# Order of half-height matmuls in the GLA and RWKV mixers, and a full-height last product in FFN down

## The chip, the cores and the metric

The kernel runs on one NeuronCore of a Trainium2 chip. A core has five engines with a queue each: TensorE (PE, matmuls; its weight loads are shown apart as PEld), VectorE (DVE), ScalarE (ACT), GpSimd (POOL) and SyncE (SP, which here only issues DMAs). Matmuls write to PSUM, 8 banks of 128 x 512 float32; DVE and ACT read from there. The metric is the device time of one execution in microseconds. Lower is better.

## The reference

A trunk of two layers over 512 tokens with 1024 features, in float32. Layer 0 mixes with GLA (gated linear attention, chunks of 64) and RWKV-7 (chunks of 16), layer 1 with RG-LRU and mLSTM. Each layer then has a cross attention to 256 memory tokens and a gated FFN of width 2752 with a causal convolution. What the change touches, cut down:

```python
def gla_chunked(q, k, v, log_alpha):              # 4 heads, dk 64, dv 128, L = 64
    q_dec = q * exp(g); k_inv = k * exp(-g); k_end = k * exp(g_last - g)
    scores = where(causal, einsum('bhnlk,bhnsk->bhnls', q_dec, k_inv), 0.0)
    o_local = einsum('bhnls,bhnsv->bhnlv', scores, v)
    # over the chunks:  o_state = q_c @ S;  S = S * decay + k_end_c^T @ v_c
    return o_local + o_state

def rwkv7_group(...):                             # 8 heads, N = 64, L = 16
    log_w = -DECAY * sigmoid(w0 + tanh(w_lr) @ w2)
    a = sigmoid(a0 + a_lr @ a2)
    # per chunk: masked products of (a_dec, r_dec) with (b_inv, k_inv), a triangular solve, a scan

def conv_glu_ffn(xn, w_up, conv_w, conv_b, w_down):   # D_FF = 2752 = 21 * 128 + 64
    u, gt = split(xn @ w_up)
    return (silu(causal_dwconv(u)) * gt) @ w_down
```

## The kernel before, in words

Activations lie with features on partitions and the 512 tokens along the free dimension, in blocks of 128 features. A dense product takes a weight block through `wload` (L240 on): one DMA on SP's queue into a ring of three `raw` tiles, then ACT makes a high part `wh` and DVE a low part `wl`, in rings of two. `dense` multiplies both with the high and low parts of the operands (`xs`), three float32r products of 128 x 128 by 128 x 512 for each k block. These go to the PSUM pool `mm` (three banks). All other products are plain float32 and go to the pool `ax` (five banks); each float32 product is two records in the trace. Every product but the transposes is issued on line 209, so the tile names tell them apart.

The program is written as one stream of operations. A scheduler puts them on the engines' queues by data, free buffers and its own estimate of time, the written order being the priority. So dense products of a later step can stand between the products of an earlier one.

- **FFN down** (`down`, L371 on). The 22 blocks of the hidden layer are multiplied in three parts of 8, 8 and 6. The last block has only 64 real rows; its operand holds the high part on rows 0 to 63 and the low part on rows 64 to 127, and the weights' rows are there twice. So one product with `wh` makes hi\*hi and hi\*lo, and one with 64 rows of `wl` makes lo\*hi. In each layer that happens once for each of 8 output blocks; the last one of layer 1 is done in two halves of 256 tokens.
- **GLA** (`gla`). Two heads share a tile of 128 partitions (`qd`, `ki`): head `e` of pair `p` lies on rows 64e to 64e + 63. Scores (L690 on): for each head four products over 64 rows, 128 x 128, into one `ax` bank, then a masked copy on DVE into `SC`. State (L698 on): products of 64 x 64 x 128 into `us`, and a recurrence on DVE into `S`. Outputs (L714 on): for each of 4 heads one bank `o`; for each of four blocks of 128 tokens a full-height product of `v` with `SC`, then up to two half-height ones of `S` with `qd`, 64 tokens each. Then the head's norm: a square on ACT, a product with `ones_h`, Ln and Exp on ACT, a multiply on DVE.
- **RWKV** (`rwkv`, loop over `p` from L790). For each pair of heads: three blocks of the projection, the two low-rank products with `w2a2` (rows 0 to 63 for the decay, rows 64 to 127 for `a`), a chain on ACT and DVE, and the pair products (L838 on): for two groups of four chunks and each half `e`, four products over 64 rows into one bank, two masked multiplies on DVE from it, then four transposes. `during(p)` puts GLA's gate blocks and the memory's norm behind each turn. After the loop DVE solves the triangular systems.

The buffers of GLA are given back when its last head is done. The buffer of `w2a2` comes after that, and its load stands on SP's queue ahead of the later weights.

Of the kernel before, what the change touches and what calls it, by code (L numbers as in the profile page):

```python
# [17 lines left out]
P = 128  # L18
T = 512
# [123 lines left out]
class Trunk:  # L143
    def __init__(self, ctx, tc, I):
# [19 lines left out]
        for n, v in (("d", 1.0 / D), ("h", 1.0 / P)):  # L164
            t = con.tile([P, P], F32, name="ones_" + n)
            nc.gpsimd.memset(t, v)
            self.ones[n] = t
        # keeps the tensor engine at its full clock while the first loads are on their way
        warm = self.mm.tile([P, T], F32, name="mm")
# [21 lines left out]

# [1 line left out]
    def tt(self, out, a, b, op, eng=None):  # L193
# [17 lines left out]
    def conv(self, out, u, w):  # L211
        """Causal convolution of a padded tile (data from column 4); w: the taps, then the bias."""
        n = len(w) - 1
        self.act(out, u[:, 4:], AF.Identity, scale=w[n - 1], bias=w[n])
        for i in range(n - 2, -1, -1):
            d = n - 1 - i
            self.stt(out, u[:, 4 - d:T + 4 - d], w[i], out, ALU.mult, ALU.add)
# [4 lines left out]
    def split(self, pool, a):  # L222
        """hi and lo parts of a: their sum is a, and both are exact in float32r."""
        hi, lo = self.pair(pool)
        n = a.shape[0]
        self.act(hi[:n], a, AF.Copy)
        self.tt(lo[:n], a, hi[:n].bitcast(F32), ALU.subtract)
        return hi, lo

    def exp_ln(self, after=None):  # L230
        """Have the table set with both exp and ln loaded (after an instruction of ScalarE)."""
        name = "natural_log_exp_and_others"
        if after is None:
            self.nc.scalar.preload_act_table_set(name)
        else:
            with self.tc.issue_after(after.ins):
                self.nc.scalar.preload_act_table_set(name)

# [1 line left out]
    def wload(self, src, kb, m):  # L240
# [11 lines left out]
    def dense(self, ps, W, X, first=True, last=True):  # L252
        """ps += W^T X over the k blocks of W and X, each in hi and lo parts."""
        wh, wl = W
        n = len(X)
        for k, (xh, xl) in enumerate(X):
            self.mmul(ps, wh[:, k], xh, first and k == 0, False)
            self.mmul(ps, wh[:, k], xl, False, False)
            self.mmul(ps, wl[:, k], xh, False, last and k == n - 1)
# [8 lines left out]
    def half(self, name, j, k0, X, h):  # L268
        """h += the products over k blocks k0 to k0 + 3."""
        W = self.wload(self.I[name][:, j, k0:k0 + 4], 4, P)  # L270
        ps = self.mm.tile([P, T], F32, name="mm")
        self.dense(ps, W, X)
        self.add(h, h, ps)

    # ---- RMS norm: gains into the operands, 1/rms left to the consumer --
    def rstd_of(self, pool, acc, n, name, ring):
# [19 lines left out]
class Norm:  # L296
# [28 lines left out]
    def bc(self):  # L325
        """1/rms along the tokens, on all partitions."""
        if self.b is None:
            self.b = self.K.rstd_of(self.small, self.acc, self.n, "rstd", self.ps)
        return self.b

    def tok(self):
        """1/rms with the tokens on partitions."""
        if self.t is None:
# [4 lines left out]
def ffn(K, l, nm, h, feed, out=None):  # L338
    nc, X = K.nc, nm.X
    cv = lambda t, j: K.v(f"ffn_conv{l}", t * NFF + j)  # L340
    with ExitStack() as es:
# [29 lines left out]
        def down(ps, W, c, s=slice(0, T)):  # L371
# [3 lines left out]
            else:  # L375
                K.dense(ps, W, g[:-1], False, False)
                K.mmul(ps, W[0][:, 5], g[-1][0], False, False)
                K.mmul(ps, W[1][:64, 5], g[-1][0][:64], False, True)

# [104 lines left out]
def memory_norm(K, sm):  # L484
    """The normalised memory, [feature, m], two blocks of features to a tile."""
    nc = K.nc
# [32 lines left out]
def memory_k(K, l, X, stage):  # L519
    """k^T [feature, m] of layer l into DRAM; X in two parts, or whole."""  # L520
    nc = K.nc
# [17 lines left out]
def memory_v(K, l, X, stage):  # L539
    """v [m, feature] of layer l into DRAM."""  # L540
    nc = K.nc
# [23 lines left out]
def reset_mask(K, pool, n):  # L565
    """Ones, with a zero where each chunk starts."""
    t = pool.tile([P, 8, n], F32, name=f"reset{n}")
# [5 lines left out]
def stacked_weights(K, src, n, m, w, queue):  # L573
    """n columns (with zeros up to m) in hi parts, and in lo parts from column m on."""
    raw = K.wr.tile([P, 1024], F32, name="raw")[:, :KD * m]
# [8 lines left out]
def stacked_step(K, ps, w, n, k, x):  # L584
    """The products of block k: hi and lo parts of the columns land on rows from 0 and from m."""
    xh, xl = x
# [6 lines left out]
def gla(K, nm, wga, wk, squares, after, Y):  # L593
    nc, X = K.nc, nm.X
    with ExitStack() as es:
# [79 lines left out]
        for half in range(2):  # L675
# [12 lines left out]
            for t in range(4):  # L688
                K.act(v[:, t, half * 256:(half + 1) * 256], ps[t // 2][:, t % 2], AF.Copy, scale=rt[:, t:t + 1])
        for p in range(2):  # L690
            for e in range(2):
                r = slice(64 * e, 64 * e + 64)
                ps = K.ax.tile([P, 4, P], F32, name="ax")
                for t in range(4):
                    ts = slice(t * P, (t + 1) * P)
                    K.mmul(ps[:, t], ki[p][r, ts], qd[p][r, ts])
                nc.vector.copy_predicated(out=SC[2 * p + e], mask=gm.to_broadcast([P, 4, P]), data=ps)
        S = gp.tile([P, 2, 7, P], F32, name="S")  # L698
        for p in range(2):
            us = {}  # L700
            for c in range(7):
# [10 lines left out]
                else:  # L712
                    K.stt(S[:, p, c], S[:, p, c - 1], sd[p][:, c, 63:64], u, ALU.mult, ALU.add)
        for h in range(4):  # L714
            p, r = h // 2, slice(64 * (h % 2), 64 * (h % 2) + 64)
            o = K.ax.tile([P, T], F32, name="ax")
            for t in range(4):
                ts = slice(t * P, (t + 1) * P)
                K.mmul(o[:, ts], v[:, t, h * P:(h + 1) * P], SC[h][:, t], t == 0, False)
                for c in (2 * t, 2 * t + 1):  # L720
                    if c:
                        cs = slice(c * 64, c * 64 + 64)
                        K.mmul(o[:, cs], S[r, p, c - 1], qd[p][r, cs], False, c == 7)
            sq = gt.tile([P, T], F32, name="sq")
# [19 lines left out]
def shifted(K, pool, name, ps, rstd, i, out=None):  # L744
    """Token shift of a projected block: p + (prev - p) * mu."""
    u = K.u[i % 2]
# [8 lines left out]
def sigmoid(K, out, a, **kw):  # L755
    """1 / (1 + exp(-a)); scale and bias as they go into exp."""
    K.act(out, a, AF.Exp, **kw)
# [4 lines left out]
def rwkv(K, X, rstd, Y, during, after):  # L762
# [3 lines left out]
    with ExitStack() as core:  # L766
# [11 lines left out]
        with ExitStack() as es:  # L778
# [11 lines left out]
            for p in range(4):  # L790
                r = shifted(K, K.qr, "xs", K.block("w_rw", p, X), rstd, p)
                k = shifted(K, K.qr, "xs", K.block("w_rw", 4 + p, X), rstd, 4 + p)
                v = shifted(K, K.qr, "xs", K.block("w_rw", 8 + p, X), rstd, 8 + p, vp[:, 64:576])
                ps = K.ax.tile([P, T], F32, name="ax")
                K.mmul(ps, w2a2[0:64, p * P:(p + 1) * P], wa[0:64])
                e1 = tp.tile([P, 8, 65], F32, name="e1")
                nc.gpsimd.memset(e1[:, :, 0:1], 0.0)
# [9 lines left out]
                K.act(sdt[:, :, p:p + 1], e1[:, :, 64:65], AF.Copy)  # L807
                ps = K.ax.tile([P, T], F32, name="ax")
                K.mmul(ps, w2a2[64:128, p * P:(p + 1) * P], wa[64:128])
                a = tp.tile([P, T], F32, name="a")  # L810
                sigmoid(K, a, ps, scale=-1.0, bias=neg[:, 4 + p:5 + p])
                kn = tp.tile([P, T], F32, name="kn")
# [25 lines left out]
                for c0 in (0, 4):  # L838
                    cs = slice(c0, c0 + 4)
                    rm = K.rmask.rearrange("p (o m) -> p o m", o=1).to_broadcast([P, 4, P])  # L840
                    for e in range(2):
                        ps = K.ax.tile([P, 4, P], F32, name="ax")
                        for c in range(4):
                            K.mmul(ps[:, c], bk[R[e], c0 + c].rearrange("p a l -> p (a l)"),
                                   stk[e][R[e], p, c0 + c])
                        K.mul(BB[R[e], p, cs], ps[R[e]], rm[R[e]])
                        K.mul(stk[e][R[1 - e], p, cs], ps[R[1 - e]], rm[R[1 - e]])
                    ps = K.ax.tile([P, 4, P], F32, name="ax")
# [114 lines left out]
def lru(K, X, rstd, Y, after, gate):  # L963
    nc = K.nc
    with ExitStack() as es:
# [3 lines left out]
        nc.sync.dma_start(out=wg, in_=K.I["w_lg"])  # L969
        # softplus(-lam) = max(-lam, 0) + log1p(e), e = exp(-|lam|); log1p(e) = 2 atanh(e / (2 + e))  # L970
        o0 = VEC["lru_lambda"][0]
# [66 lines left out]
def mlstm(K, nm, hp):  # L1038
    nc, X = K.nc, nm.X
    with ExitStack() as es:  # L1040
# [18 lines left out]
        ch = [slice(P * c, P * c + P) for c in range(4)]  # L1059
        # gate rows: heads on partitions 0-3 (input) and 32-35 (forget)  # L1060
        wif = stacked_weights(K, K.I["w_if"][:, 0], 36, 64, K.wh.tile([P, 1024], F32R, name="wh"), nc.sync)
# [150 lines left out]
def trunk(tc, I, out):  # L1212
    nc = tc.nc
    with ExitStack() as ctx:
# [63 lines left out]
        for l in range(2):  # L1278
# [23 lines left out]
            else:  # L1302
# [3 lines left out]
                def finish(s, ps):  # L1306
                    """The last block of the residual for some tokens, their norm, and their output."""
                    r = nt.tile([P, T], F32, name="nsq")[:, 0:256]
# [29 lines left out]
```

## Time and profile before

| | us |
|---|---|
| median of 3 runs | 1587.1 |
| lowest and highest run | 1581.17, 1588.97 |
| profiled execution: span from its first to its last instruction | 1579.1 |
| PE busy in it | 1550.2 |
| DVE busy | 937.3 |
| ACT busy | 667.6 |

The page gives the profiled execution by its span alone. The runs shown are 2.1 to 9.9 us longer than that span; what lies around the span, ahead of the first and behind the last instruction, is within this difference. The mean granted clock of TensorE over the span is 0.992 of full speed. A share of busy time is a mean over stages; PE's records overlap, so the length of a stretch of PE is read from the starts of its records.

### The profile page before, as it was taken

To read this page: it belongs to the slowest core of one execution; us is meant where nothing else is said; L and a number is where in the kernel's file an instruction comes from. 1 tells how busy PE (TensorE), PEld (TensorE's weight loads), DVE (VectorE), ACT (ScalarE), POOL (GpSimd) and SP (SyncE) were. 2 spreads that over 40 slices of the span, in tenths; PEclk is the share of its full clock that TensorE was granted. 3 is DMA by queue.
4 is the path that set the end of the run, shared out by engine and by line. 5 is a ranking of instruction groups with operands and counts; after the bars stand their busy time and mean duration, and the time that the engine had idled before them with its cause. 6 is when DMAs were issued, how large, how long until landed. Compare 5 with 4: busy or idle time off the path is not lost. (4 is left out here: it accounts for less than half of the span.)

```text
span 1579.1 us, 19936 instructions
## 1 busy us (share of the span) xinstructions
PE 1550.2 (98%) x7953; PEld 1249.7 (79%) x7953; DVE 937.3 (59%) x1382; ACT 667.6 (42%) x1058; POOL 23.3 (1%) x62
## 2 busy tenths in 40 slices
PE   8999998999999999999999999999999999999997
PEld 6877777786888888888877767788888888888776
DVE  6447989646555756655633375777567655565233
ACT  5345542436444543333322257565445333333221
POOL 2000000011000000000000000000000000000000
PEclk9999999899999999999999999999999999999999
DMA  5212225335341333333333330325214333333332
GB/s 175 68 47 94 67 72 150 120 90 195 117 131 36 100 107 93 94 96 104 91 97 90 91 109 28 91 63 153 74 47 120 95 99 100 94 93 97 94 93 77
DMA packets 50173, 152.17 MB, mean 96 GB/s; under 512 B 5504, under 2 KB 8864, under 8 KB 50080
## 3 DMA queue, kind: packets, MB, share of 16 engines
q1 hardware_dynamic: 45664, 142.87, 30.0%
q10 hardware_dynamic: 3536, 5.38, 0.9%
q0 software_dynamic: 880, 2.66, 0.5%
q8 instruction: 62, 1.02, 0.3%
q14 instruction: 31, 0.25, 0.0%
HBM read 144.59 MB, written 6.29 MB: 96 GB/s over the span
## 5 line engine op out<-in xcount | busy, mean ns | idle before, releaser
L209 PE MATMUL mm<-xs,wh 128*128 128x512 f32 (+1 forms) x3627 | 1114.8, 388 | 3.2 <-DVE upad L194 1.4
L209 PEld LDWEIGHTS mm<-xs,wh 128*128 128x128 f32 x3627 | 670.6, 188 | 150.6 <-issue 10.4
L209 PE MATMUL mm<-xs,wl 128*128 128x512 f32 (+2 forms) x1814 | 702.6, 387 | 0.3 <-DVE wl L194 0.3
L206 ACT ACTIVATE wh<-raw 128x1024 fp32r<-128x1024 f32 (+2 forms) x273 | 264.9, 970 | 537.6 <-PE mm L209 438.7
L194 DVE TENSOR_TENSOR wl<-raw,wh 128x1024 fp32r<-128x1024 f32 (+2 forms) x272 | 302.5, 1112 | 192.7 <-ACT wh L206 191.8
L209 PEld LDWEIGHTS mm<-xs,wl 128*128 128x128 f32 (+1 forms) x1814 | 341.0, 188 | 77.7 <-issue 7.6
L194 DVE TENSOR_TENSOR upad<-mm,rstd 128x512 f32<-128x512 f32 x66 | 45.5, 690 | 111.2 <-PE mm L209 108.0
L194 DVE TENSOR_TENSOR h<-h,mm 128x512 f32<-128x512 f32 (+1 forms) x73 | 49.4, 677 | 72.5 <-PE mm L209 72.4
L194 DVE TENSOR_TENSOR g<-mm,rstd 128x512 f32<-128x512 f32 (+1 forms) x44 | 30.4, 692 | 76.0 <-PE mm L209 75.9
L209 PE MATMUL mm<-wh,xs 128*128 128x256 f32 (+1 forms) x256 | 67.3, 350 | 0.7 <-ACT wh L206 0.7
L203 DVE SCALAR_TENSOR_TENSOR c<-upad,vec,c 128x512 f32<-128x512 f32 (+1 forms) x88 | 65.9, 749 | 3.3 <-ACT c L206 1.8
L206 ACT ACTIVATE c<-c 128x512 f32<-128x512 f32 (+1 forms) x44 | 27.8, 632 | 87.1 <-DVE c L203 87.1
L209 PEld LDWEIGHTS mm<-wh,xs 128*128 128x128 f32 x256 | 44.5, 192 | 8.0 <-ACT wh L206 2.3
L209 PE MATMUL mm<-wl,xs 128*128 128x256 f32 (+1 forms) x128 | 44.6, 348 | 4.5 <-DVE wl L194 4.5
L206 ACT ACTIVATE xs<-g 128x512 fp32r<-128x512 f32 (+1 forms) x44 | 27.8, 633 | 27.2 <-DVE g L194 27.2
L206 ACT ACTIVATE c<-upad,vec 128x512 f32<-128x512 f32 (+1 forms) x44 | 35.3, 802 | 1.5 <-DVE upad L194 1.5
L206 ACT ACTIVATE e<-ax,mx,scl 128x256 f32<-128x256 f32 x32 | 17.8, 560 | 39.8 <-DVE mx L194 39.8
L194 DVE TENSOR_TENSOR g<-c,g 128x512 f32<-128x512 f32 (+1 forms) x44 | 30.4, 692 | 6.1 <-ACT c L206 1.4
L194 DVE TENSOR_TENSOR nacc<-nacc,nsq 128x512 f32<-128x512 f32 x45 | 32.9, 730 | 0.3
L194 DVE TENSOR_TENSOR xs<-ax,xs 128x512 fp32r<-128x512 f32 x32 | 21.3, 687 | 18.0 <-ACT xs L206 18.0
L203 DVE SCALAR_TENSOR_TENSOR xs<-h,vec,xs 128x512 fp32r<-128x512 f32 x40 | 29.9, 749 | 3.5 <-ACT xs L206 3.4
L206 ACT ACTIVATE xs<-h,vec 128x512 fp32r<-128x512 f32 x40 | 28.9, 722 | 7.3 <-DVE h L194 6.6
(349 smaller groups left out, 1248.2 us busy)
## 6 DMA issues: line engine op xcount, KB each, us to landing
raw<-in_w_up SPq DMA_DIRECT2D x86, 512.0 KB, 3.5
raw<-in_w_dn SPq DMA_DIRECT2D x32, 512.0 KB, 3.6
raw<-in_w_kk SPq DMA_DIRECT2D x16, 512.0 KB, 4.1
raw<-in_w_kv SPq DMA_DIRECT2D x16, 512.0 KB, 4.5
raw<-in_w_q SPq DMA_DIRECT2D x16, 512.0 KB, 3.8
raw<-in_w_o SPq DMA_DIRECT2D x32, 256.0 KB, 2.7
raw<-in_w_cd SPq DMA_DIRECT2D x16, 512.0 KB, 3.6
raw<-in_w_rw SPq DMA_DIRECT2D x14, 512.0 KB, 3.8
```

Source lines behind the costliest of these rows:

```text
L194: (eng or self.nc.vector).tensor_tensor(out=out, in0=a, in1=b, op=op)
L203: return self.nc.vector.scalar_tensor_tensor(out=out, in0=a, scalar=s, in1=b, op0=op0, op1=op1)
L206: return self.nc.scalar.activation(out=out, in_=a, func=f, **kw)
L209: self.last_mm = self.nc.tensor.matmul(out, lhsT=l, rhs=r, start=start, stop=stop)
```

## The change

1. FFN down: the product of `wl` with the last block uses all 128 rows of both operands.
2. GLA scores: both heads of a pair get a bank, their products alternate, and the two masked copies follow.
3. GLA outputs: a function `outputs(p)` does two heads at a time: first all full-height products of both heads, then the half-height ones, alternating between the heads.
4. RWKV: the `a` product of `w2a2` is written right behind the decay product, into a bank of its own.
5. RWKV pair products: both halves get a bank, and their products alternate.

Comments and docstrings are dropped as well. The diff, cut to what computes:

```diff
@@ ffn
-                K.mmul(ps, W[1][:64, 5], g[-1][0][:64], False, True)
+                K.mmul(ps, W[1][:, 5], g[-1][0], False, True)
@@ gla
         for p in range(2):
+            ps = [K.ax.tile([P, 4, P], F32, name="ax") for _ in range(2)]
+            for t in range(4):
+                ts = slice(t * P, (t + 1) * P)
+                for e in range(2):
+                    r = slice(64 * e, 64 * e + 64)
+                    K.mmul(ps[e][:, t], ki[p][r, ts], qd[p][r, ts])
             for e in range(2):
-                r = slice(64 * e, 64 * e + 64)
-                ps = K.ax.tile([P, 4, P], F32, name="ax")
-                for t in range(4):
-                    ts = slice(t * P, (t + 1) * P)
-                    K.mmul(ps[:, t], ki[p][r, ts], qd[p][r, ts])
-                nc.vector.copy_predicated(out=SC[2 * p + e], mask=gm.to_broadcast([P, 4, P]), data=ps)
+                nc.vector.copy_predicated(out=SC[2 * p + e], mask=gm.to_broadcast([P, 4, P]), data=ps[e])
...
+        def outputs(p):
+            os = [K.ax.tile([P, T], F32, name="ax") for _ in range(2)]
+            for e in range(2):
+                h = 2 * p + e
+                for t in range(4):
+                    ts = slice(t * P, (t + 1) * P)
+                    K.mmul(os[e][:, ts], v[:, t, h * P:(h + 1) * P], SC[h][:, t], t == 0, False)
+            for c in range(1, 8):
+                for e in range(2):
+                    r = slice(64 * e, 64 * e + 64)
+                    cs = slice(c * 64, c * 64 + 64)
+                    K.mmul(os[e][:, cs], S[r, p, c - 1], qd[p][r, cs], False, c == 7)
+            return os
+
         for h in range(4):
-            p, r = h // 2, slice(64 * (h % 2), 64 * (h % 2) + 64)
-            o = K.ax.tile([P, T], F32, name="ax")
-            for t in range(4):
-                ts = slice(t * P, (t + 1) * P)
-                K.mmul(o[:, ts], v[:, t, h * P:(h + 1) * P], SC[h][:, t], t == 0, False)
-                for c in (2 * t, 2 * t + 1):
-                    if c:
-                        cs = slice(c * 64, c * 64 + 64)
-                        K.mmul(o[:, cs], S[r, p, c - 1], qd[p][r, cs], False, c == 7)
+            if h % 2 == 0:
+                os = outputs(h // 2)
+            o = os[h % 2]
@@ rwkv
                 ps = K.ax.tile([P, T], F32, name="ax")
+                psa = K.ax.tile([P, T], F32, name="ax")
                 K.mmul(ps, w2a2[0:64, p * P:(p + 1) * P], wa[0:64])
+                K.mmul(psa, w2a2[64:128, p * P:(p + 1) * P], wa[64:128])
...
-                ps = K.ax.tile([P, T], F32, name="ax")
-                K.mmul(ps, w2a2[64:128, p * P:(p + 1) * P], wa[64:128])
                 a = tp.tile([P, T], F32, name="a")
-                sigmoid(K, a, ps, scale=-1.0, bias=neg[:, 4 + p:5 + p])
+                sigmoid(K, a, psa, scale=-1.0, bias=neg[:, 4 + p:5 + p])
...
+                    ps = [K.ax.tile([P, 4, P], F32, name="ax") for _ in range(2)]
+                    for c in range(4):
+                        for e in range(2):
+                            K.mmul(ps[e][:, c], bk[R[e], c0 + c].rearrange("p a l -> p (a l)"),
+                                   stk[e][R[e], p, c0 + c])
                     for e in range(2):
-                        ps = K.ax.tile([P, 4, P], F32, name="ax")
-                        for c in range(4):
-                            K.mmul(ps[:, c], bk[R[e], c0 + c].rearrange("p a l -> p (a l)"),
-                                   stk[e][R[e], p, c0 + c])
-                        K.mul(BB[R[e], p, cs], ps[R[e]], rm[R[e]])
-                        K.mul(stk[e][R[1 - e], p, cs], ps[R[1 - e]], rm[R[1 - e]])
+                        K.mul(BB[R[e], p, cs], ps[e][R[e]], rm[R[e]])
+                        K.mul(stk[e][R[1 - e], p, cs], ps[e][R[1 - e]], rm[R[1 - e]])
```

## Rows read from the trace of the kernel before

**Rows 1.** The page's first part: busy us, share of the span, records.

```profile
PE 1550.2 (98%) x7953; PEld 1249.7 (79%) x7953; DVE 937.3 (59%) x1382; ACT 667.6 (42%) x1058; POOL 23.3 (1%) x62
```

**Rows 2.** Waits of PE: line, released by; us in total, times, longest.

```profile
PE ax L209 <- DVE sc L697: 0.6, 1, 0.6
```

**Rows 3.** Chain that ended last, in order of time: start, us, what.

```profile
1216.36 347.35 PE mm L209 x1552
```

**Rows 4.** Groups with shapes apart, PE: rows x columns, operand, count | busy us, mean ns | idle.

```profile
L209 PE MATMUL mm<-xs,wl 64*128 64x512 f32 x15 | 7.4, 492 | 0.0
...
L209 PE MATMUL mm<-xs,wl 64*128 64x256 f32 x2 | 0.8, 384 | 0.0
```

**Rows 5.** Timeline of PE, end of a block of FFN down: start us, us, record.

```profile
817.43 0.39 PE L209 MATMUL mm<-xs,wl 128*128 128x512 f32 x1
817.67 0.40 PE L209 MATMUL mm<-xs,wh 128*128 128x512 f32 x1
818.00 0.49 PE L209 MATMUL mm<-xs,wl 64*128 64x512 f32 x1
818.42 0.73 PE L209 MATMUL mm<-xs,wh 128*128 128x512 f32 x2
```

**Rows 6.** Timeline of PE, outputs of GLA's second head.

```profile
80.77 0.39 PE L209 MATMUL ax<-sc,v 128*128 128x128 f32 x2
81.08 0.43 PE L209 MATMUL ax<-qd,S 64*128 64x64 f32 x2
81.44 0.49 PE L209 MATMUL ax<-sc,v 128*128 128x128 f32 x2
81.86 0.66 PE L209 MATMUL ax<-qd,S 64*128 64x64 f32 x4
...
84.45 0.50 PE L209 MATMUL mm<-xs,wh 128*128 128x512 f32 x1
```

**Rows 7.** Timeline of PE, transposes of full height in RWKV.

```profile
123.89 1.20 PE L825 MATMUL ax<-cmat,vp 128*128 128x128 f32 x9 [0.27 <-DVE vp L203]
```

**Rows 8.** Timeline of PE, the low-rank products of the first p.

```profile
120.51 1.13 PE L209 MATMUL ax<-wa,w2a 64*128 64x512 f32 x4
121.57 1.12 PE L209 MATMUL ax<-kn,cmat 128*128 128x512 f32 x2
```

**Rows 9.** Timeline of PE, GLA scores.

```profile
65.09 2.82 PE L209 MATMUL ax<-qd,ki 64*128 64x128 f32 x32
```

**Rows 10.** Timeline of DVE, masked copies of the scores.

```profile
68.04 1.93 DVE L697 COPY_PREDICATED sc<-gmask,ax 128x512 f32<-128x512 uint8 x3
```

**Rows 11.** Timeline of PE, pair products of the third p, both groups.

```profile
196.91 1.94 PE L209 MATMUL ax<-stk,bk 64*128 64x128 f32 x16 [0.26 <-DVE bk L194]
...
199.37 1.71 PE L209 MATMUL ax<-stk,bk 64*128 64x128 f32 x16
```

**Rows 12.** Busy in the first p's pair products: PE, PEld, DVE, ACT, POOL, clock.

```profile
134.00:142.00 8.00, 7.44 (x52) 5.96 (x52) 7.88 (x13) 1.87 (x3) 0.00 (x0) 1.00 0.01 2
```

**Rows 13.** Timeline of PE, a wait in the second p.

```profile
155.05 0.47 PE L209 MATMUL mm<-xs,wh 128*128 128x512 f32 x1 [1.36 <-DVE upad L194]
```

**Rows 14.** Busy behind the first head's outputs, columns as in rows 12.

```profile
76.90:80.40 3.50, 3.50 (x10) 2.48 (x10) 0.00 (x0) 0.60 (x1) 0.00 (x0) 0.51 0.02 5
```

**Rows 15.** Timeline of SP, the load of w2a2.

```profile
100.21 0.33 SPq L782 DMA_DIRECT2D w2a<-in_w_w2a  x1
```

**Rows 16.** Timeline of PE, a dense product among GLA's state products.

```profile
69.78 0.51 PE L209 MATMUL mm<-xs,wh 128*128 128x512 f32 x1
70.22 0.43 PE L209 MATMUL ax<-v,kt 64*64 64x128 f32 x5
```

**Rows 17.** Timeline of PE, from one block of the projection to the next.

```profile
98.43 0.39 PE L209 MATMUL mm<-xs,wl 128*128 128x512 f32 x1
98.66 0.62 PE L209 MATMUL mm<-xs,wh 128*128 128x512 f32 x2
```

## The prediction

> **What bounds the kernel now.** I read the page first, then the waits of PE, then the chain that ended last, and only then single stretches. PE is busy for 1550.2 of 1579.1 us, so only 28.9 us of the span are free of matmul work [rows 1]. The waits say the same of the place that the change touches first: only one wait of PE, 0.6 us, is for the masked scores of GLA [rows 2]. The chain runs for its last piece, 347.35 us long, through nothing but dense products of the second FFN [rows 3]. So PE's stream sets the time nearly everywhere, and an edit that shortens the stream is worth its full length, unless the next product then waits for DVE, ACT or a load. The start times of the matmuls tell how long the stream is; busy time does not, since matmuls overlap.
>
> **FFN down.** The edit removes no instruction: 17 products that use 64 rows [rows 4] now use 128. Around one of them the starts are 817.43, 817.67, 818.00 and 818.42, and the two after it last 0.73 together, so the second of these starts at about 818.42 + 0.73 - 0.40 = 818.75 [rows 5]. The steps are 0.24 (full to full), then 0.33, 0.42, 0.33. Three steps of full height are 3 x 0.235 = 0.70, and these take 1.08: a half-height product between full ones costs 0.38 us. Fifteen of width 512 give 15 x 0.38 = 5.7. Two of width 256 stand in the tail; by the same steps I give them 0.3 each, bounds 0.2 and 0.4. The term is **-6.3**, bounds -6.0 and -6.6. In the second FFN the chain stays on PE all through [rows 3], so nothing that loads or splits weights is late there; the first FFN has the same code and blocks. A rule of the Trainium skill speaks against this edit: "TensorE: Matmul & The Clock Gate", section "Why this matters for your kernels", says that a product over 32 rows takes as long as one over 128; by that alone the edit is worth nothing, and the sum is -8.9. The same skill's "TensorEngine Tiling (Array Packing)", Key Properties, says that changing the tiling mode drains the engine, and that agrees with the 0.33 and 0.42.
>
> **GLA outputs (line 714 on).** Before, each head runs four rounds of one full-height product (two records each, as every fp32 product here) and up to two half-height ones. A round of the second head starts at 80.77, 81.08, 81.44, 81.86: two full records take 0.31 or 0.42 up to the next height, two half ones 0.36, four half ones last 0.66; the head as a whole takes 84.45 - 80.77 = 3.68 us [rows 6]. Four heads: 14.7. (The first also holds four products of the state; they stay.) After, a pair of heads runs 16 full records, then 28 half-height ones whose row halves alternate. Full-height fp32 records of this width go at (1.20 - 0.27) / 8 = 0.12 at most, 0.11 once running [rows 7]: 16 x 0.11 + 0.1 for the change of height = 1.86. Half-height ones go at 0.112 in one half: (0.66 - 0.27 - 0.16) / 2 [rows 6]. That two halves run at once is seen where they already alternate: four half-height records of width 512 take 121.57 - 120.51 = 1.06, as long as two full-height ones (last 1.12 together) [rows 8]. So 28 are 14 steps: 14 x 0.112 + 0.15 for the two changes of height = 1.7. A pair of heads: 3.57 for 7.36; two pairs save **-7.6**. Bounds: -4.4 if halves don't overlap (14 more steps a pair, 3.1 us in all), -8.0 at best. Nothing of it is hidden: PE runs without a wait in all four heads, and the dense products that fill the waits for the norms stay as they are. If those run out, PE waits for ACT (rival A).
>
> **GLA scores.** 32 records last 2.82 from the first start to the last end, less than 32 x 0.112 = 3.6: the halves overlap already in part [rows 9]. Alternating, the last of 16 steps starts after 0.2 + 14 x 0.112 and lasts 0.27: 2.04, so 0.78 less on PE. But DVE takes until 68.04 + 1.93 for the last three masked copies [rows 10], and PE waits there already [rows 2]. I take 0; bounds 0 and -0.8.
>
> **RWKV low-rank products (w2a2).** The moved product costs nothing and brings nothing: the four records already start in pairs [rows 8], since the order written in the program is not the order on the engine. Bounds 0 and 0. The other accumulator is held no longer for it.
>
> **RWKV pair products (line 838 on).** A group of 16 lasts 1.94 or 1.71 [rows 11]; alternating, the last of 8 steps starts after 0.2 + 6 x 0.112 and lasts 0.27: 1.14. Eight groups, four of each kind, save 4 x (0.80 + 0.57) = 5.5 us of PE. Here DVE sets the pace: it is busy 7.88 of 8.00 us in the stretch of the first p [rows 12], and a little later PE waits 1.36 us for DVE [rows 13]; the second p is alike. The first half's result is not ready earlier than before, since its own records keep their pace. After the fourth p, DVE solves the triangular systems, so PE's time is not the end there either. Only the third p is followed by a long run of PE without such a wait. I take its 1.37, rounded down for a DVE that has little to spare there too: **-1.3**; bounds 0 and -5.5.
>
> **Clock.** In one stretch of 3.5 us behind the first head's outputs the granted clock is 0.51, so the lower level, 1.2 GHz; what ran just before was small products only [rows 14]. At half the clock 3.5 us lose at most 1.7. The change takes away many of the small products but packs the rest; I take 0, bounds -1.7 and +1.7 (one stretch less or more).
>
> **Sum.** -6.3 - 7.6 + 0 + 0 - 1.3 + 0 = -15.2 us. The profiled span becomes 1579.1 - 15.2 = 1563.9. The runs shown are 2.1 to 9.9 us above that span, their median 8.0; with the same 8.0 the forecast is 1571.9.
>
> **Rivals.** (A) GLA's gain comes to nothing at its end. The load of w2a waits for the buffers of GLA and is issued only at 100.21, and all later weights stand behind it in SP's queue [rows 15]. The four heads' norms run one after another on ACT and PE; if with two heads arriving at a time the last one ends as late as before, the 7.6 are lost, and what is left is -6.3 to -7.6: 1580. For it: the load really is the last to come there. Against: PE is full all through it, and two weight blocks are at hand as filler.
> (B) PE's gain counts in every RWKV group: -5.5 for -1.3, so 1567.7. For it: PE is nearly full there too. Against: [rows 12, 13].
> (C) Alternate halves don't run at once in short products. Then outputs give 4.4, RWKV nothing: -10.7, 1576.4. Against: [rows 8].
> (D) The other side: the scheduler, which orders each engine's queue, puts a dense product between alternate halves. One such stands between the state products: it starts at 69.78, some 0.2 after the half before it (a change of height), and the half after it at 70.22 [rows 16]: 0.63 apart for 0.11 + 0.235; with the overlap lost that is 0.29 + 0.22 = 0.5 each. There are 8 + 14 + 32 = 54 pairs; if every one is split, 27 us come on: 1599, slower. It decides from 30 split pairs on. For it: three dense products stand among the state products. Against: among the outputs there is none inside a head.
> (E) The 0.38 belongs to the end of an accumulation, not to the height, so FFN gains nothing: -8.9, 1578.2. Against: where a block of the RWKV projection ends at full height (98.43) the next one's first product starts 0.23 later [rows 17]. (It is what the skill's rule on rows, named above, would give.)
>
> **Chances.** Forecast 0.58, A 0.16, B 0.12, C 0.05, D 0.06, E 0.03. A measurement of this kernel tells about 0.5% from no change, 7.9 us: faster means below 1579.2, slower above 1595. Faster: 0.55 of the forecast (its own range is 1566 to 1578, and the runs spread by 7.8 us), all of B, 0.05 of C, 0.02 of E and 0.03 of A make 0.77. Slower: D, 0.05. The rest, 0.18, is the same. The range leaves out D, and the far half of A's and B's spread: 1563 to 1583.
>
> **What would show it.** FFN: all steps 0.235 at the end of a block. Outputs: 16 records of the masked scores in a row, then 28 in pairs that start together, some 3.6 us a pair of heads. w2a loaded 7 to 8 us earlier, at 92 to 93. RWKV: groups of 16 last 1.1 to 1.2 us, and PE's waits for DVE grow by 0.5 to 1.3 each in the first, second and fourth p. It is wrong if w2a's load doesn't move, if dense products stand between the halves, or if the starts of the halves go one by one.

## The result and the profile after

The changed kernel takes 1570.93 us (median of four runs, 1567.24 to 1575.38) for 1587.29 beside it: ratio 0.990, 95% interval 0.9871 to 0.9928. In the first round of experiments it took 1571.49 for 1584.83, ratio 0.9913 (0.9883 to 0.9944). The forecast was 1571.9. The profiled execution took 1569.39 us with a span of 1567.6.

The page's first part answers [rows 1]: PE is busy 16.0 us less.

```profile
PE 1534.2 (98%) x7953; PEld 1243.7 (79%) x7953; DVE 938.6 (60%) x1382; ACT 666.9 (43%) x1058; POOL 23.3 (1%) x62
```

FFN down, the timeline of PE at the end of a block, answers [rows 5]: start, duration, record. The last product of the block is the one at 810.97; it now has 128 rows, and the steps around it are 0.23, 0.24 and 0.23.

```profile
810.50 0.39 PE L209 MATMUL mm<-xs,wl 128*128 128x512 f32 x1
810.73 0.40 PE L209 MATMUL mm<-xs,wh 128*128 128x512 f32 x1
810.97 0.39 PE L209 MATMUL mm<-xs,wl 128*128 128x512 f32 x1
811.20 0.63 PE L209 MATMUL mm<-xs,wh 128*128 128x512 f32 x2
```

The long piece of the chain [rows 3] is the same 1552 records, 2.97 us shorter: seven products of width 512 and one of width 256 at 0.38 and 0.3 are 2.96.

```profile
1208.04 344.38 PE mm L209 x1552
```

GLA, timeline of PE, answers [rows 9], [rows 2] and [rows 6]. The 32 scores last 2.06 us for 2.82, and then PE waits 0.57 and 0.26 for the masked copies, where it waited 0.6 once. The second pair of heads begins at 80.53 and is done at 84.12: 3.59 us for the 7.36 of two heads. Sixteen full records stand in a row, then 28 half-height ones in 1.78 us, and no dense product among them.

```profile
65.78 2.06 PE L209 MATMUL ax<-qd,ki 64*128 64x128 f32 x32
67.76 0.44 PE L209 MATMUL ax<-v,kt 64*64 64x128 f32 x4
68.77 0.44 PE L209 MATMUL ax<-v,kt 64*64 64x128 f32 x4 [0.57 <-DVE sc L698]
69.47 0.95 PE L209 MATMUL ax<-v,kt 64*64 64x128 f32 x12 [0.26 <-DVE sc L698]
...
80.53 1.95 PE L209 MATMUL ax<-sc,v 128*128 128x128 f32 x16
82.41 1.78 PE L209 MATMUL ax<-qd,S 64*128 64x64 f32 x28
84.12 0.73 PE L209 MATMUL mm<-xs,wh 128*128 128x512 f32 x2
```

On SP the load of w2a2 goes out 10.8 us earlier than in [rows 15]:

```profile
89.41 0.33 SPq L792 DMA_DIRECT2D w2a<-in_w_w2a  x1
```

RWKV, timeline of PE, answers [rows 13] (first line) and [rows 11]: both groups of the third turn, then the fourth turn up to PE's wait. The second group of a turn has shrunk from 1.71 to 1.16; the first of the third turn still lasts 1.94. The wait at the end of the first turn is 2.08 for 1.36, that of the fourth 1.35 for 0.39 (the lines of the kernel before for the fourth turn follow).

```profile
146.68 0.71 PE L209 MATMUL mm<-xs,wh 128*128 128x512 f32 x2 [2.08 <-DVE upad L194]
...
189.94 1.94 PE L209 MATMUL ax<-stk,bk 64*128 64x128 f32 x16 [0.27 <-DVE bk L194]
192.40 1.16 PE L209 MATMUL ax<-stk,bk 64*128 64x128 f32 x16
...
229.66 1.85 PE L209 MATMUL ax<-stk,bk 64*128 64x128 f32 x16 [1.41 <-DVE bk L194]
232.02 1.16 PE L209 MATMUL ax<-stk,bk 64*128 64x128 f32 x16
237.71 1.56 PE L209 MATMUL mm<-xs,raw 128*128 128x256 f32 x6 [1.35 <-ACT kvs L206]
```

```profile
237.20 1.85 PE L209 MATMUL ax<-stk,bk 64*128 64x128 f32 x16 [1.40 <-DVE bk L194]
...
244.84 0.70 PE L209 MATMUL mm<-xs,raw 128*128 128x256 f32 x2 [0.39 <-ACT kvs L206]
```

The windows (columns as in [rows 12]) answer [rows 14]: behind the outputs the clock is full. Another stretch, behind the 2.08 us wait of the first turn, now has 0.50, the lower level of 1.2 GHz.

```profile
76.90:80.40 3.50, 3.50 (x29) 2.34 (x26) 0.00 (x0) 1.61 (x3) 0.00 (x0) 1.00 0.02 5
147.40:150.80 3.40, 3.40 (x9) 2.64 (x9) 3.34 (x5) 0.73 (x1) 0.00 (x0) 0.50 0.01 2
```

### The profile page after: what moved, and what is told of

Its sections match the earlier page's. It is cut to its first block, busy times and chain, and to the rows that moved or that the text cites. A ratio compares the mean times of both kernels' runs of the same rounds, so it can differ in the third digit from the quotient of the medians.

```text
span 1567.6 us, 19931 instructions
## 1 busy us (share of the span) xinstructions
PE 1534.2 (98%) x7953; PEld 1243.7 (79%) x7953; DVE 938.6 (60%) x1382; ACT 666.9 (43%) x1058; POOL 23.3 (1%) x62
## 5 line engine op out<-in xcount | busy, mean ns | idle before, releaser
L209 PE MATMUL mm<-xs,wl 128*128 128x512 f32 (+1 forms) x1814 | 700.6, 386 | 0.6 <-DVE wl L194 0.5
L209 PEld LDWEIGHTS mm<-xs,wl 128*128 128x128 f32 x1814 | 341.4, 188 | 71.9 <-issue 1.9
L209 PEld LDWEIGHTS mm<-wl,xs 128*128 128x128 f32 x128 | 24.8, 194 | 9.3 <-DVE wl L194 6.3
```

The costliest lines, as they stand in the source:

```text
L209: self.last_mm = self.nc.tensor.matmul(out, lhsT=l, rhs=r, start=start, stop=stop)
```

## The experiments

Twelve runs, each beside the kernel before on the same chip. Single runs of one kernel spread by 10 us and more, and most of that goes with the mean granted clock of the run: within the kernels, a run's time falls by 1.23 us for each 0.001 of mean clock (one slope fitted to all their runs). So the table gives the median as it is, and beside it the difference of the means with every run brought to a clock of 0.991 by that slope, with its standard error. The kernel before has 87 runs on four chips, median 1585.3, mean clock 0.9896; taken against the runs of its own chip alone, a difference changes by at most 0.7 us. A kernel can also move the clock itself (0.9931 in one row), and the last column takes that out: it tells what the work costs, not what a user sees.

| kernel | runs | median us | ratio to before (95%) | mean clock | to before at equal clock, us |
|---|---|---|---|---|---|
| FFN down alone | 12 | 1578.27 | 0.9957 (0.9934 to 0.9979) | 0.9902 | -6.4 +- 0.4 |
| outputs by pairs alone | 12 | 1576.14 | 0.9952 (0.9932 to 0.9972) | 0.9903 | -8.2 +- 0.3 |
| pair products alone | 12 | 1588.25 | 1.0024 (1.0004 to 1.0044) | 0.9877 | +0.2 +- 0.4 |
| whole change | 6 | 1571.49 | 0.9913 (0.9883 to 0.9944) | 0.9907 | -13.8 +- 0.3 |
| half height in the middle | 12 | 1586.16 | 0.9996 (0.9972 to 1.0019) | 0.9894 | +0.5 +- 0.4 |
| outputs, halves in blocks | 9 | 1575.74 | 0.9928 (0.9901 to 0.9955) | 0.9931 | -5.8 +- 0.3 |
| outputs, heights mixed | 12 | 1577.99 | 0.9953 (0.9930 to 0.9976) | 0.9906 | -6.1 +- 0.3 |
| scores alone | 12 | 1587.69 | 1.0006 (0.9979 to 1.0033) | 0.9884 | +0.5 +- 0.4 |
| FFN and outputs only | 5 | 1570.75 | 0.9911 (0.9889 to 0.9933) | 0.9902 | -14.3 +- 0.5 |
| before, a multiply on GpSimd | 10 | 1591.27 | 1.0044 (1.0026 to 1.0061) | 0.9882 | +4.0 +- 0.3 |
| after, a multiply on GpSimd | 6 | 1573.88 | 0.9930 (0.9907 to 0.9953) | 0.9888 | -12.9 +- 0.5 |
| after, an operation on ACT | 6 | 1570.37 | 0.9903 (0.9885 to 0.9921) | 0.9908 | -13.3 +- 0.4 |

**FFN down alone** (its hunk of the change, nothing else).

> Only the FFN-down edit; everything else as before. Theory: a half-height product between full-height ones costs 0.38 us more than three full steps, so 15 x 0.38 + 2 x 0.3 go: -6.3 us against before (bounds -6.0 to -6.6), half of it in each layer; the four steps at the end of a block are then 0.235 each. Rival E (the 0.38 belongs to the end of an accumulation, not to the height): 0 us, and the steps at the end of a block stay 0.33 and 0.42. No other place of the trace may move by more than a stretch of low clock explains (about 2 us each).

Measured: -6.4 at equal clock, the term of the prediction. All steps at the ends of blocks are 0.23 to 0.24. Rival E falls here, and the next kernel says where the cost sits.

**The half-height product kept, but moved.** It tests height against the end of an accumulation:

```diff
-                K.dense(ps, W, g[:-1], False, False)
-                K.mmul(ps, W[0][:, 5], g[-1][0], False, False)
-                K.mmul(ps, W[1][:64, 5], g[-1][0][:64], False, True)
+                K.dense(ps, W, g[:2], False, False)
+                K.mmul(ps, W[1][:64, 5], g[-1][0][:64], False, False)
+                K.dense(ps, (W[0][:, 2:], W[1][:, 2:]), g[2:-1], False, False)
+                K.mmul(ps, W[0][:, 5], g[-1][0], False, True)
```

> FFN down with the half-height product kept, but issued behind the second of the last part's five full k blocks; the accumulation now ends with a product of full height. All else as before. Theory (the height costs): 0 us against before, plus or minus a stretch of low clock; the steps 0.33, 0.42, 0.33 stand in the middle of the part and the steps at its end are 0.235. Rival E (the end of an accumulation costs): the slow steps stay at the end of the block, where the last full-height product now takes 0.33 to 0.42, and the moved product's steps are 0.235.

Measured: +0.5 +- 0.4, nothing. The slow steps went with the product. In PE's timeline of this kernel the two records at 820.37 are the last full product before it and the half-height one itself:

```profile
820.14 0.39 PE L209 MATMUL mm<-xs,wh 128*128 128x512 f32 x1
820.37 0.82 PE L209 MATMUL mm<-xs,wl 128*128 128x512 f32 x2
821.12 0.73 PE L209 MATMUL mm<-xs,wh 128*128 128x512 f32 x2
821.68 0.39 PE L209 MATMUL mm<-xs,wl 128*128 128x512 f32 x1
```

From 820.37 to 821.12 are 0.75 for two products, and to 821.68 another 0.56 for two: 1.31 for four where four full steps are 0.93. The 0.38 belongs to the change of height.

**Outputs by pairs alone.**

> Only the outputs of GLA by pairs of heads; scores, RWKV and FFN as before. Theory: two pairs of heads take 3.57 us each for 7.36, so -7.6 us at the last output and at the end of the program (plus or minus about 2 us for one stretch of low clock more or less), and the load of w2a goes out 7 to 8 us earlier. Rival A (the gain is lost at the end of GLA, where the norms of the heads and the load of w2a follow): outputs are shorter, but w2a's load and the first product of RWKV's second turn come as late as before, total 0. Rival C (halves don't overlap): -4.4 us.

Measured: -8.2 +- 0.3. The second pair of heads stands as in the changed kernel: it starts at 80.05, its half-height products at 81.92, and it is done at 83.63, 3.58 us. w2a2's load goes out at 88.93, and the first group of pair products starts at 125.54 for 134.56. The gain isn't lost at GLA's end: rival A falls.

**The two halves of that gain.** The first kernel keeps the full-height products apart and puts the half-height ones in blocks; the second alternates but goes from height to height in each round. The first diff is against `outputs(p)` of the change; the second, cut down, shows the products of its own `outputs(p)`:

```diff
-            for c in range(1, 8):
-                for e in range(2):
+            for e in range(2):
+                for c in range(1, 8):
```

> GLA outputs two heads at a time, the 16 full-height records first, but the 28 half-height ones in two blocks of 14 (first head, then second) instead of alternating. Theory (both parts of the gain count): half-height records in one half go at 0.112 each, so 28 take 3.1 us instead of 14 steps' 1.6; a pair of heads takes 3.59 + 1.57 = 5.2 us and the kernel gains 4.4 us on before, 3.1 less than with alternation. Rival (overlap brings nothing; only the changes of height do): a pair takes 3.6 us and the gain is the full 7.6.

```diff
+            for t in range(4):
+                for e in range(2):
+                    K.mmul(os[e][:, ts], v[:, t, h * P:(h + 1) * P], SC[h][:, t], t == 0, False)
+                for c in (2 * t, 2 * t + 1):
+                    for e in range(2):
+                        if c:
+                            K.mmul(os[e][:, cs], S[r, p, c - 1], qd[p][r, cs], False, c == 7)
```

> GLA outputs two heads at a time, halves alternating, but each round of 128 tokens goes from full height to half height and back, eight changes of height a pair of heads instead of two. Theory: a round takes 4 full records (about 0.55 us up to the next height) and 4 steps of paired halves (about 0.58); with the short first round a pair takes 4 x 0.55 + 0.36 + 3 x 0.58 = 4.3 us, so the kernel gains 6.1 us on before, 1.5 less than with the full-height products apart. Rival (changes of height are free): a pair takes 3.6 us, gain 7.6. Rival C (halves of different rows don't run at once): 5.9 us a pair, gain 3.0.

PE's timeline of the second pair of heads, in blocks:

```profile
80.88 1.95 PE L209 MATMUL ax<-sc,v 128*128 128x128 f32 x16
82.75 2.94 PE L209 MATMUL ax<-qd,S 64*128 64x64 f32 x28
85.63 1.98 PE L209 MATMUL ax<-sq,ones_h 128*128 128x512 f32 x4
```

and with heights mixed:

```profile
80.93 0.61 PE L209 MATMUL ax<-sc,v 128*128 128x128 f32 x4
81.47 0.44 PE L209 MATMUL ax<-qd,S 64*128 64x64 f32 x4
81.84 0.71 PE L209 MATMUL ax<-sc,v 128*128 128x128 f32 x4
82.48 0.66 PE L209 MATMUL ax<-qd,S 64*128 64x64 f32 x8
...
85.54 0.73 PE L209 MATMUL mm<-xs,wh 128*128 128x512 f32 x2
```

In blocks a pair takes 85.63 - 80.88 = 4.75 us; alternating brings it to 3.59, so the overlap is worth 1.16 a pair and 2.3 us in all (expected 3.1: at the border between the blocks some records do overlap). Mixed, a pair takes 85.54 - 80.93 = 4.61 (expected 4.3); the six changes of height that the change saves are worth 1.0 a pair, 2.0 in all. At equal clock the kernels stand at -5.8 and -6.1, which is the -8.2 less these. Rival C falls, and so does the thought that one of the two ideas alone would do. By the clock as it fell, though, the kernel in blocks isn't slower than the alternating one (1575.74 for 1576.14): its nine runs have a mean clock of 0.9931, and why they do is not shown.

**Scores alone.**

> Only the GLA scores alternate their halves. Theory: the 32 records last 2.0 instead of 2.8 us, but PE then waits for the masked copies on DVE 0.8 us longer; 0 us at the end of GLA and of the program (plus or minus a stretch of low clock). Rival: -0.8 us, because the copies start earlier as well.

Measured: +0.5 +- 0.4. In its trace the scores start at 65.44 and the first dense product behind the waits at 70.02, 4.58 us; before it was 65.09 to 69.78 [rows 9, 16], 4.69. Of 0.78 us, 0.11 is left.

**Pair products alone.**

> Only the pair products of RWKV alternate their halves; the rest as before. Theory (DVE is the limit there): PE's groups of 16 shrink from 1.94 and 1.71 to about 1.14 us, 5.5 us in all, but PE then waits longer for DVE; 0 to -1.3 us of it stays at the end of RWKV's last turn. Rival B (PE is the limit): -5.5 us at the end, and PE's waits for DVE as before.

Measured: slower by its ratio, and nothing at equal clock (+0.2 +- 0.4). The windows say where most of its clock went in the profiled run: some 14 us at half clock from 72 to 85, which is GLA. This kernel's first difference from the kernel before in PE's order comes behind 139. The stretch from 70 to 100, first of this kernel, then of the one with outputs by pairs:

```profile
70.00:100.00 30.00, 30.00 (x150) 21.56 (x146) 6.55 (x16) 6.03 (x10) 0.00 (x0) 0.77 0.05 17
```

```profile
70.00:100.00 30.00, 30.00 (x202) 23.23 (x203) 13.99 (x28) 14.81 (x21) 1.22 (x4) 1.00 0.15 42
```

Another 3.4 us at half clock follow PE's wait at the end of the first turn. A stretch like it stands there in all five profiles with alternating pair products, and in two of the nine without. So a part of what the equal-clock column takes out may be this edit's own doing; no run separates it.

Rival B falls too, and PE's gain of 5.5 us isn't even there: only the second group of a turn shrinks, by 0.55 us. In the first, DVE makes the operands `bk` of the second half last, and that half can't start before. The timeline of DVE in the third turn shows it, of the changed kernel, then of the kernel before. The first of the two multiplies releases the first half; the second ends at 190.62, 0.68 us after the group's start at 189.94, and eight records of the second half then take it to 1.94 in any order. In the kernel before it ends at 197.58, 0.67 us after the start at 196.91, so its own trace held this already.

```profile
189.21 1.41 DVE L194 TENSOR_TENSOR bk<-xs,e 64x512 f32<-64x512 f32 x2
```

```profile
196.18 1.40 DVE L194 TENSOR_TENSOR bk<-xs,e 64x512 f32<-64x512 f32 x2
```

**The whole change, and FFN with outputs only** (the other three edits undone).

> The whole change, beside its parts on one chip. If the parts add up: the FFN's -6.3, the outputs' -7.6 and 0 to -1.3 of the pair products make -13.9 to -15.2 us against before; with the profiled waits at the end of RWKV's fourth turn, where the gain of the third one was already given back, rather -14 to -16 by the times measured so far (1570.9 for 1587.3). If the parts hinder each other, the sum of the three alone is larger than this by several us.

> The changed kernel without three of its parts: GLA's scores, the low-rank products and the pair products of RWKV are as before; only FFN down's full-height last block and the outputs by pairs of heads are in. Theory (the other three parts bring nothing to the end): the same time as the changed kernel, that is -14 to -15 us against before (-6.4 and -8.2 as the two parts alone gave at equal clock, and the clock as it falls). Rival (the pair products bring 1.3 us or more once GLA is shorter, as predicted for the third turn): 1 to 5 us longer than the changed kernel.

Measured: -13.8 +- 0.3 and -14.3 +- 0.5, no difference. The parts add up: -6.4 - 8.2 + 0.2 + 0.5 = -13.9.

**A multiply on GpSimd**, in the kernel before and in the changed one:

```diff
-                    K.mul(stk[e][R[e], p, :, 64:128], c8(r)[R[e]], e1[R[e], :, 1:])
+                    K.mul(stk[e][R[e], p, :, 64:128], c8(r)[R[e]], e1[R[e], :, 1:], nc.gpsimd)
```

> The kernel before, with one multiply of RWKV's turns (r by e1 into stk, 8 instructions of 684 ns on DVE) moved to GpSimd; nothing else. It takes 5.5 us off DVE in the stretch where DVE is said to be the limit. On GpSimd it will take longer: its multiplies of 128 x 512 take 1523 ns, so some 3 us a turn for 1.4. Theory (DVE is the limit of RWKV's turns): PE's waits for DVE shrink, and 1 to 4 us go at the end of the loop if the two products come before the pair products are due on GpSimd; 0 if GpSimd's own 3 us stand in the way. Rival (PE is the limit): 0, with the waits as before.

> The changed kernel with the same multiply on GpSimd. Theory (DVE hides what the pair products save on PE): with 5.5 us less on DVE part of the 5.5 us of PE time shows; the gain over the changed kernel is larger than that of the same edit on the kernel before, 2 to 5 us, and the waits of PE for DVE at the ends of the first, second and fourth turn (2.08, 1.55, 1.35 us in the changed kernel) shrink. Rival (the chain through GpSimd takes DVE's place): 0 or slower, with the waits now ended by GpSimd's multiply. If PE were the limit: 0, waits as they are.

Measured: slower by 4.0 us, and by 0.9 +- 0.6 in the changed kernel. In the first and fourth turn the edit took the wrong work off DVE. The first turn in the kernel before with the edit, timelines of GpSimd, of DVE and of PE, one line each:

```profile
127.95 2.45 POOL L194 TENSOR_TENSOR stk<-xs,e 64x512 f32<-64x512 f32 x2 [24.84 <-ACT e L206]
```

```profile
129.58 1.36 DVE L203 SCALAR_TENSOR_TENSOR kn<-xs,vec,kn 128x512 f32<-128x512 f32 x1 [2.38 <-ACT kn L206]
```

```profile
136.82 1.89 PE L209 MATMUL ax<-stk,bk 64*128 64x128 f32 x16 [1.42 <-issue]
```

DVE did those multiplies while it waited for `kn` (the normalised key) from ACT; without them it waits 2.38 us, and in the kernel before they left only this wait:

```profile
127.93 0.75 DVE L203 SCALAR_TENSOR_TENSOR kn<-xs,vec,kn 128x512 f32<-128x512 f32 x1 [0.29 <-ACT kn L206]
```

And `kn` itself takes 1.36 for 0.75 with GpSimd at work beside it; PE starts 0.6 later for that (a wait of 1.42 for 0.84). In the second and third turn DVE hardly waits for `kn` (0.11 us or less), and GpSimd is done before it. There the scheduler moved dense products: the second turn holds 148 records of PE for 142 and lasts 31.53 us for 29.83. So these runs don't tell whether DVE behind `kn` is the limit, which they were meant to, and what makes up the rest of the 4.0 us was not followed.

**An operation behind `kn`, moved to ACT** in the changed kernel (`ka1` is 1 minus the factor, made once):

```diff
-                nc.vector.tensor_scalar(out=a, in0=a, scalar1=-1.0, scalar2=K.v("rwkv_k_a", p),
-                                        op0=ALU.add, op1=ALU.mult)
-                K.stt(k, a, 1.0, k, ALU.add, ALU.mult)
+                K.act(a, a, AF.Identity, scale=K.v("rwkv_k_a", p), bias=ka1[:, p:p + 1])
                 bk = tp.tile([P, 8, 2, 64], F32, name="bk")
                 for e in range(2):
                     K.mul(bk[R[e], :, e], c8(kn)[R[e]], e2[R[e]])
+                K.mul(k, k, a)
+                for e in range(2):
                     K.mul(bk[R[e], :, 1 - e], c8(k)[R[e]], e2[R[e]])
```

> The changed kernel with one operation of each RWKV turn moved from DVE to ACT: (a - 1) times its factor, 0.48 us on DVE, becomes a scale and a bias on ACT (some 0.6 us), and a multiply replaces the fused one that follows. Unlike the multiply that went to GpSimd, it stands behind kn, inside the row of DVE work that leads to the pair products and through the masked multiplies. Theory (that row on DVE is the limit): 0.48 us a turn, 4 turns: -1 to -1.9 us against the changed kernel, with the turns shorter by 0.3 to 0.5 each. Rival (the turn is set by something else, ACT's chain from the low-rank product to kn or the stream of dense products): 0, or up to 1 us slower if a split of a weight block now stands ahead of the pair products on DVE.

Measured: -13.3 +- 0.4 for -13.8, no gain. The windows of the second turn, from its first group to that of the third (columns as in [rows 12]): the kernel before, the changed kernel, and this one.

```profile
167.08:196.91 29.83, 28.45 (x142) 21.79 (x142) 29.43 (x43) 16.93 (x29) 0.11 (x1) 1.00 0.24 71
```

```profile
160.11:189.94 29.83, 27.77 (x142) 20.98 (x142) 29.43 (x43) 17.05 (x29) 0.11 (x1) 1.00 0.24 71
```

```profile
162.05:190.90 28.85, 26.88 (x138) 20.23 (x139) 28.08 (x41) 17.77 (x30) 0.11 (x1) 1.00 0.25 73
```

In the kernels whose DVE work is untouched that turn is 29.82 to 29.84, with alternating pair products and without. DVE is busy for 29.43 of it, so there DVE is the limit, and what PE saves in its second group is worth nothing. In this run the turn is 1.0 us shorter, but that isn't the worth of the moved operation (0.48 us): DVE is busy 1.35 us less and PE has four records fewer. One split of weights (1.22 us on DVE) has left the turn, three for four. From the last norm of GLA to the first group there is one more, six for five, and that stretch is 0.7 us longer. The rival's second clause came true there, and the sum is nothing. No kernel beats the changed one by more than its error.

## Why the prediction was right, and where it wasn't

- **FFN down**, -6.3: right in size and cause. Steps of 0.235 everywhere, 2.97 us in the last chain, -6.4 in the run by itself. By the Trainium skill's rule that a product over 32 rows takes as long as one over 128 ("TensorE: Matmul & The Clock Gate", "Why this matters for your kernels") the edit would be worth nothing. Here 0.38 us go with a half-height product alone among full ones, and the run with the product moved shows it; what such products take among their own kind wasn't tested at this width. The Trainium skill's "TensorEngine Tiling (Array Packing)", "Key Properties", says that a change of the tiling mode drains the engine; the longer steps around that product agree.
- **GLA outputs**, -7.6: right. A pair takes 3.59 for a forecast of 3.57. Two pairs save 2 x 3.77 = 7.5 by the trace; of the -8.2 +- 0.3 at the end 0.7 is not explained. Both parts of the working, apart and at once, were shown each by a run. The forecast that the dense products that fill in stay as they are was wrong: before, four stood ahead of each head's norm, now three stand ahead of both. So the norms came 10.8 us earlier, w2a2's load at 89.41 and not at 92 to 93, and some 2 us of it went back to dense products that were now left for later: from the last norm to the first pair products are 39.76 us for 37.48.
- **Scores**, 0: right, for the reason given; 0.11 is left of 0.78.
- **w2a2**, 0: by itself not run. Without it and two other edits the time is the same.
- **Pair products**, -1.3: the term that was mis-sized; it measured +0.2 +- 0.4. The step that failed is "a group of 16 lasts 1.94 or 1.71; alternating, ... 1.14": it counted the first groups as if only the order of the halves held them, and DVE held them with the operand of the second half. So the third turn gained 0.57 (40.29 to 39.72 between the first groups of the third and fourth) and not 1.37, and the fourth gave most of it back. Alternating ends both halves late, so DVE begins its row of eight multiplies later after the group's start: 231.33 - 229.66 = 1.67 in the changed kernel, where it was 238.47 - 237.20 = 1.27 before. The forecast "the first half's result is not ready earlier" was too kind; it is later by 0.40. PE's wait behind that grew by 0.96: the 0.55 that PE saved in its second group, and these 0.40. (In the first and third turn the scheduler put a split of weights, 1.22 us, into that room ahead of the multiplies.) Timeline of DVE in the fourth turn, after, then before:

```profile
231.33 0.68 DVE L194 TENSOR_TENSOR bb<-ax,cmat 64x512 f32<-64x512 f32 x1 [0.32 <-PE ax L209]
```

```profile
238.47 0.68 DVE L194 TENSOR_TENSOR bb<-ax,cmat 64x512 f32<-64x512 f32 x1
```

- **DVE as the cover of RWKV**: the waits grew in the first, second and fourth turn by 0.72, 0.57 and 0.96, as forecast (0.5 to 1.3). Of the first, the edit's share is not shown: the other profiles without alternating pair products have 1.72 to 2.57 us there, those with it 2.05 to 2.29. That DVE is the limit is shown for the second turn. Over the whole first turn it is busy for 27.43 of 32.52 us in the kernel before, over the third for 34.81 of 40.29, so the 7.88 of 8.00 in [rows 12] holds for the part around the pair products alone.
- **Clock**, 0: not settled for this kernel. Its six runs have 0.9907 for 0.9896, worth 1.4 us by the slope, but the difference of 0.0011 has an error of 0.0013. Over all rows of the table, outputs by pairs have 0.9908 (56 runs) and outputs head by head 0.9893 (145), a difference of 0.0015 +- 0.0004. All six profiles with outputs head by head have a stretch at half clock between 70 and 100 us (mean clock of the 30 us 0.77 to 0.94); all eight with outputs by pairs have 1.00. What brings it on stays open. In two of the six the clock falls at 71 to 72, among the products of the state and ahead of the first output, so there the outputs' short rounds don't explain it; and the kernel with heights mixed, which keeps short rounds, has 1.00.
- **Sum**: -13.8 at equal clock, -13.9 by parts, for a forecast of -15.2. The pair products and the scores gave 2.0 less than forecast, the outputs and the FFN 0.7 more. That the median of 1570.93 lies within 1 us of the forecast 1571.9 is partly luck: the forecast started from 1587.1, the median of three runs, where 87 runs have 1585.3, and these 1.8 us cover the 1.4 that the sum had too much.
- **Rivals**: A, B, C and E each fell by a run; D by the trace, where no dense product stands between alternate halves.

## What to carry to other kernels

On PE, look at the steps between starts around a lone product of fewer rows: the cost lies in these steps, and padding it to the full height or gathering such products takes it away. Alternating halves pays where PE is the limit and both halves are ready; where a second engine reads the results in a row, it made the first result late and saved nothing here. Before taking work off an engine that seems to be the limit, see whether that work stood in one of its waits. When a stretch gets shorter, count its records first: the scheduler may only have moved work out of it.

## What the runs showed of the hardware

- A step from full to half height and back costs 0.38 us around one product of width 512. A change of columns alone doesn't show it: in PE's timeline of the kernel before, eight full-height records with 100 and 36 columns in turn last 2.02 us, the last of them 0.39, so a step is 1.63 / 7 = 0.23, as between equal ones.

```profile
913.05 2.02 PE L209 MATMUL mm<-xs,wh 128*36 128x512 f32 x8
```

- Two multiplies of 64 x 512 on GpSimd took 2.45 us where DVE takes 1.39, and a DVE operation with two inputs beside them took 1.36 for 0.75. In the turns of the same trace where GpSimd was done before it, it took 0.75. The Trainium skill ("SBUF — State Buffer", "Who interferes with whom") says that a DVE instruction with two inputs in SBUF contends with a GpSimd instruction that reads SBUF, over a pair of ports that both share; the trace agrees with that.
- Half-height records in two blocks overlap a little at the border: 28 take 2.88 us up to the next product, where 28 at 0.112 would be 3.1.
- A run's mean granted clock differs between runs of one kernel (0.981 to 0.995 for the kernel before) and explains most of their spread.
